# A hybrid decoder layer in float32: the order of high and low weight parts in the query and key projections

## The chip, the cores and the metric

The kernel runs on one core of a Trainium2 chip, as one launch. The metric is the device time of one execution in microseconds. The kernel before took 1053.3 us as the median of 3 runs (1052.99 to 1053.78). Engines are named as in the profile: PE is TensorE, DVE VectorE, ACT ScalarE, POOL GpSimd, SP the engine whose queue issues most DMAs.

## The reference

One decoder layer on x of 256 tokens by 2048 channels, all float32. The part that matters here is the token mixer:

```
h = rmsnorm(x, pre_mix_g)
q_a, k_a, v_a, q_b, k_b, v_b, f_b = split(h @ w_in)
o_a = swa_sink_attention(q_a, k_a, v_a, sinks)       # 16 query heads of 64, 2 key heads, window 128
o_b = forgetting_attention(q_b, k_b, v_b, cumsum(log_sigmoid(f_b + b_forget)))  # 16 heads of 64
x = x + rmsnorm(concat(rmsnorm(o_a), rmsnorm(o_b)) @ w_out, post_mix_g)
```

A channel mixer follows: an up-projection to 2 x 5632 columns, a causal convolution of width 3, GELU of one half times the other, a down-projection, a post-norm and a residual.

## The kernel before, in words

**Float32 as pairs.** TensorE multiplies operands that hold a rounded high part, and a low part carries the rest. A weight w is split by ScalarE (a cast to the high part, `w_split` or `w_high`, line 119) and VectorE (w minus high, the low part, line 122). The activations are held as `hT`: 16 slices of 128 channels, each 512 columns wide, 256 tokens' high parts and then their low parts. A product needs three terms: high weight by high and by low activations (one matmul of 512 columns, line 263), and low weight by high activations (one of 256 columns, line 270, added to the second half of the bank). The two halves of the bank are summed when it is evacuated (`evac_sum`, lines 448 to 450: a ScalarE copy, a VectorE add, a GpSimd multiply with the row norms), and the sum is split again into a high and a low part (`split`, lines 320 and 321).

**Projections with held weights.** `proj_T` computes 256 output columns of a weight matrix for all tokens, transposed, in two banks. The 2048 rows of the weight make four units of 512 rows. A unit is one load of 512 KB into one of 5 `raw` buffers, and one of 5 `wpair` buffers for its two parts. `get(u)` loads and splits a unit at its first use. `high(u)` issues 8 matmuls of 512 columns, `low(u)` 8 of 256. The argument `runs` is the order: its entries are, in turn, units whose high parts and units whose low parts are multiplied. After each unit of each run `tick()` is called, so a projection has eight ticks in either order. `w_parts` also sets where in the pair buffer the low part lies: `LOW[unit[0] % period[0]] * 4` columns behind column 1024, with `LOW = (14, 4, 4, 4)` and a period of 2 or 4 units.

**Who calls it.** In order of the program: two first projections written out by themselves (key and value of the SWA group, first query), three SWA query projections (`proj_T(w_in, g * 256, b2)`), the V projections of the FoX group (untransposed, line 317), then four times a FoX query projection and a FoX key projection. The second projection of `w_up` calls `proj_T` with an order of its own, `LONG`. All other projections of `w_up` use `proj_S` (line 300), in which every matmul has 256 columns.

**What sets the order of the work.** TensorE's order is the program's (`manual_schedule`). The attention of each pair of heads is hung into it by ticks: `later(n, f)` calls f at the n-th tick from now. `attend` hangs up four pieces, `tables`, `scores`, `transposes` and `pv`. For a SWA pair they come at the ticks of `stages(6 + 8 * g, m)`, for a FoX pair at those of `stages(5, m)`, that is 5, 9 + 4m and 13 + 4m ticks on, m being the pair's place in the projection (both pairs of a projection are scored at the same tick). `scores` (line 483) needs the split queries and keys and two banks of the attention pool, of which there are four; `transposes` (line 518) needs the softmax (lines 489 on VectorE, 501 on ScalarE, 508 on VectorE); `pv` (lines 527 and 529) needs the split probabilities `ph` and `pl`. Also hung on ticks: the transposition of the SWA values (`v_T`, tick 3, line 617; its split `vpa` frees its bank), and the cumulative sum of the forget gates (`cumsum`, tick 7 of the first FoX query projection), whose rows come back through DRAM as `cb` (line 582) for `tables`.

The order on ScalarE, VectorE, GpSimd and in SP's DMA queue is not written out in this part of the kernel; it is worked out when the program is built, from the program's order and from what is estimated to be ready. On the chip each of these queues runs in the order so fixed.

## Time and profile before

| | |
|---|---|
| median of 3 runs | 1053.3 us |
| the profiled execution | 1053.3 us |
| its span, first to last instruction | 1051.4 us |
| granted TensorE clock, mean | 0.997 |
| busy: PE, DVE, ACT, POOL | 1040.0, 837.2, 626.9, 166.5 us |
| `proj_T` with the default order | 32.7 to 73.3 us and 128.4 to 236.7 us |

How to read the lines. In a timeline a line gives start and length in us, the engine, the source line, the operation, what it writes and reads, the shape and how many instructions were merged; in brackets, the idle time of its engine before it and what ended that. Lengths of PE lines overlap, since matmuls are pipelined: the next line's start is where a stretch really ends. In the chain of waits a line gives start, length and the piece of work that the end of the program goes back to at that time. In the page's first part a line gives each engine's busy time, its share of the span and its instructions.

### The profile page before, as it was taken

The page shows a single profiled execution, that of the slowest core. Times are in us where ns is not written, and L with a number is a line of the kernel's source. Part 1 is how long each engine was busy: PE and PEld are TensorE (multiplying, and loading weights), DVE is VectorE, ACT ScalarE, POOL GpSimd, SP SyncE. Part 2 cuts the span into 40 slices and gives each one's busy share as a digit, 9 for nine tenths or more (in the row PEclk, how much of TensorE's full clock was granted, in tenths as well). Part 3 has the DMA queues.
Part 4 walks back from the last instruction along what each step waited for, and adds up shares of the span by engine and source line. Part 5 has one row for each costly group of instructions (what it writes and reads, how often), then busy time and mean ns, then how long its engine had stood idle before and what let it go on. Part 6 is the DMA issues. An engine that isn't in the chain of part 4 may idle for free.

```text
span 1051.4 us, 19021 instructions
## 1 busy us (share of the span) xinstructions
PE 1040.0 (99%) x7240; PEld 958.0 (91%) x7240; DVE 837.2 (80%) x1365; ACT 626.9 (60%) x1025; POOL 166.5 (16%) x210
## 2 busy tenths in 40 slices
PE   9999999999999999999999999999999999999996
PEld 7899988888888999999999888899999999988886
DVE  5999877887467888888877988967788777799783
ACT  6777757667557655555555655645565455566561
POOL 3253245441122210100000000000111000000023
PEclk9999999999999999999999999999999999999998
DMA  8645557555874878888875886777677776767783
GB/s 292 199 129 168 182 159 214 164 180 171 294 248 153 255 252 294 287 264 273 283 232 170 263 269 226 244 233 239 220 235 246 226 244 219 236 216 246 244 306 115
DMA packets 187335, 238.98 MB, mean 227 GB/s; under 512 B 8268, under 2 KB 154988, under 8 KB 186348
## 3 DMA queue, kind: packets, MB, share of 16 engines
q1 hardware_dynamic: 186924, 237.37, 69.5%
q8 instruction: 57, 0.93, 0.3%
q10 hardware_dynamic: 320, 0.40, 0.1%
q14 instruction: 34, 0.28, 0.1%
HBM read 221.86 MB, written 15.75 MB: 226 GB/s over the span
## 4 chain that ended last, share of the span: by engine, by line
PE 90%; DVE 4%; ACT 2%; DMA 1%; POOL 1%; issue 1%; SPq 0%; DVEq 0%; POOLq 0%; ACTq 0%
PE bank_att L300 23%; PE bank_acc L300 21%; PE bank_acc L1072 15%; PE bank_acc L317 12%; PE bank_acc L263 5%; PE bank_att L1072 5%; PE bank_acc L270 3%; DVE wpair L122 1%; PE bank_att L317 1%; POOL scr L450 1%; PE bank_att L518 1%; DMA raw<-in_w_in_dram 1%; PE bank_att L483 1%; PE bank_att L527 1%; DMA x_in<-in_x_dram 1%
## 5 line engine op out<-in xcount | busy, mean ns | idle before, releaser
L122 DVE TENSOR_TENSOR wpair<-raw,wpair 128x1024 fp32r<-128x1024 f32 (+3 forms) x317 | 383.6, 1225 | 116.9 <-ACT wpair L119 115.8
L119 ACT CAST wpair<-raw 128x1024 fp32r<-128x1024 f32 (+3 forms) x316 | 320.3, 1032 | 155.6 <-issue 62.6
L300 PE MATMUL bank_att<-hT,wpair 128*128 128x256 f32 x2112 | 241.2, 276 | 0.0
L300 PEld LDWEIGHTS bank_att<-hT,wpair 128*128 128x128 f32 x2112 | 240.4, 188 | 0.2
L300 PE MATMUL bank_acc<-hT,wpair 128*128 128x256 f32 x1920 | 219.2, 276 | 0.0
L300 PEld LDWEIGHTS bank_acc<-hT,wpair 128*128 128x128 f32 x1920 | 218.3, 188 | 0.0
L1072 PE MATMUL bank_acc<-wpair,G 128*128 128x512 f32 x636 | 153.5, 389 | 0.0
L1072 PEld LDWEIGHTS bank_acc<-wpair,G 128*128 128x128 f32 x636 | 119.1, 188 | 24.5
L263 PE MATMUL bank_acc<-hT,wpair 128*128 128x512 f32 x384 | 94.9, 394 | 0.0
L263 PEld LDWEIGHTS bank_acc<-hT,wpair 128*128 128x128 f32 x384 | 69.5, 188 | 13.2
L317 PE MATMUL bank_acc<-wpair,oT 128*128 128x512 f32 x336 | 78.0, 391 | 0.0
L317 PEld LDWEIGHTS bank_acc<-wpair,oT 128*128 128x128 f32 x336 | 62.6, 188 | 12.8
L1030 POOL TENSOR_TENSOR s<-yy 128x128 f32<-128x128 f32 x11 | 7.5, 681 | 408.1 <-DVE yy L1019 408.1
L320 ACT CAST wpair<-raw 128x1024 fp32r<-128x1024 f32 (+1 forms) x54 | 48.0, 892 | 36.2 <-PE bank_acc L1072 17.6
L321 DVE TENSOR_TENSOR wpair<-raw,wpair 128x1024 fp32r<-128x1024 f32 (+1 forms) x54 | 55.0, 1023 | 14.3 <-ACT wpair L320 13.4
L899 ACT ACTIVATE yy<-u,cw 128x256 f32<-128x256 f32 x88 | 48.4, 596 | 20.4 <-DVE u L894 15.3
L270 PE MATMUL bank_acc<-hT,wpair 128*128 128x256 f32 x384 | 49.4, 280 | 0.0
L270 PEld LDWEIGHTS bank_acc<-hT,wpair 128*128 128x128 f32 x384 | 47.4, 188 | 1.4
L317 PE MATMUL bank_acc<-wpair,hT 128*128 128x384 f32 (+1 forms) x288 | 47.7, 321 | 0.0
L317 PEld LDWEIGHTS bank_acc<-wpair,hT 128*128 128x128 f32 x288 | 45.4, 188 | 0.1
L320 ACT CAST G<-yy 128x256 fp32r<-128x256 f32 x44 | 16.0, 406 | 46.8 <-POOL yy L1031 23.9
L901 DVE SCALAR_TENSOR_TENSOR yy<-u,cw,yy 128x256 f32<-128x256 f32 x88 | 39.1, 482 | 2.4 <-ACT yy L899 2.2
(253 smaller groups left out, 1204.9 us busy)
## 6 DMA issues: line engine op xcount, KB each, us to landing
raw<-in_w_up_dram SPq DMA_DIRECT2D x176, 512.0 KB, 4.6
raw<-in_w_down_dram SPq DMA_DIRECT2D x68, 512.0 KB, 5.1
raw<-in_w_in_dram SPq DMA_DIRECT2D x51, 512.0 KB, 5.3
raw<-in_w_out_dram SPq DMA_DIRECT2D x32, 512.0 KB, 4.1
staged<-in_w_down_dram SPq DMA_DIRECT2D x44, 256.0 KB, 5.5
t_dram<-staged SPq DMA_DIRECT2D x22, 512.0 KB, 3.2
raw<-t_dram SPq DMA_DIRECT2D x14, 512.0 KB, 3.7
raw<-in_w_in_dram SPq DMA_DIRECT2D x16, 384.0 KB, 3.4
```

What stands on the lines that cost most here:

```text
L119: i1 = act.copy(hi[:, cs], raw[:, cs])
L122: i2 = dve.tensor_tensor(lo[:, cs], raw[:, cs], hi[:, cs].bitcast(F32), op=ALU.subtract)
L263: pe.matmul(b, hi[:, a, m * P:(m + 1) * P], hT[:, kt, 0:512], start=(kt == 0), stop=(last == (0, kt)))
L270: pe.matmul(b[:, 256:512], lo[:, a, m * P:(m + 1) * P], hT[:, u * 4 + a, 0:256], start=False, stop=(last == (1, u * 4 + a)))
L300: pe.matmul(b[:, m * 256:(m + 1) * 256], ws[:, a, m * P:(m + 1) * P], hT[:, kt, i * 256:(i + 1) * 256], start=not begun, stop=last == (low ...
L317: pe.matmul(b, a, r[:, cols], start=(first and i == 0), stop=(last and i == 2))
L320: act.copy(hi, src)
L321: dve.tensor_tensor(lo, src, hi.bitcast(F32), op=ALU.subtract)
L450: pool.tensor_tensor(dst, dst, row, op=ALU.mult)
L899: act.activation(y, u[:, 2:258], AF.Identity, bias=cw[:, 3, ch:ch + 1], scale=cw[:, 2, ch:ch + 1])
L901: dve.scalar_tensor_tensor(y, u[:, 1:257], cw[:, 1, ch:ch + 1], y, op0=ALU.mult, op1=ALU.add)
L1072: pe.matmul(b, x, r, start=b not in opened and not i, stop=closes and i == 2)
```

## The change

`proj_T` takes `LONG` as its default order. The high parts of units 0 and 1 still come first and their low parts next; then come the low parts of units 2 and 3, and their high parts last. The default order had the high parts of units 2 and 3 before their low parts. The period of the low parts' shift becomes 4 in every call (it was 2 in calls with the old default), so the low part of unit 2 is shifted by 16 columns instead of 56. The call for `w_up` passed `LONG` itself and now takes it as the default, so it stays as it is. The first start and the last stop of a bank's accumulation follow from the order: the last matmul of a bank is now a wide one.

```
-    def proj_T(w, c0, banks, runs=((0, 1), (0, 1), (2, 3), (2, 3))):
+    LONG = ((0, 1), (0, 1, 2, 3), (2, 3))
+
+    def proj_T(w, c0, banks, runs=LONG):
 
         parts, last = {}, ((len(runs) - 1) % 2, KT - 1)
-        unit[0], period[0] = 0, 4 if len(runs) == 3 else 2
+        unit[0], period[0] = 0, 4
...
-    LONG = ((0, 1), (0, 1, 2, 3), (2, 3))
...
-                    proj_T(w_up, DFF + c0, bv, LONG)
+                    proj_T(w_up, DFF + c0, bv)
```

## The prediction

> **What bounds the kernel now.** I read the page first, then the chain of waits, then TensorE's timeline over the stretch that the change touches (32 to 237 us), then VectorE's and ScalarE's timelines there.

> ```profile
> PE 1040.0 (99%) x7240; PEld 958.0 (91%) x7240; DVE 837.2 (80%) x1365; ACT 626.9 (60%) x1025; POOL 166.5 (16%) x210
> ...
> PE 90%; DVE 4%; ACT 2%; DMA 1%; POOL 1%; issue 1%; SPq 0%; DVEq 0%; POOLq 0%; ACTq 0%
> ```
> ```profile
> core 0: 1051.4 us, clock 0.997
> ```

> TensorE is busy 99% of the span and makes 90% of the chain. So time is won only where its stream gets shorter, and lost wherever it waits longer; it takes its matmuls in program order, so one that waits holds all behind it. The other engines matter where they are late. In this stretch I found it late only at the first scores and at the products with V in the FoX key projections (rows below). The profiled execution took 1053.3 us, as the median of the runs did; the 1.9 us around its span of 1051.4 are not touched.

> **The change.** Eleven projections run through `proj_T` with the default order: three SWA query ones, four FoX query, four FoX key ones. Each has eight steps with a tick after each: before H0 H1 L0 L1 H2 H3 L2 L3, after H0 H1 L0 L1 L2 L3 H2 H3 (H: 8 matmuls of 512 columns, L: 8 of 256). No instruction is added or removed. Three things follow: fewer turns between wide and narrow runs, other deadlines for the low parts, and, since attention pieces are hung on tick numbers, other places for those pieces in time.

> *Turns.* These runs stand without an attention piece between them (TensorE's timeline; start, length, source line), then a piece of the chain, two unbroken up-projections of matmuls of 256 columns:

> ```profile
> 143.35 3.82 PE L263 MATMUL bank_acc<-hT,wpair 128*128 128x512 f32 x16
> 147.01 2.00 PE L270 MATMUL bank_acc<-hT,wpair 128*128 128x256 f32 x16
> 148.85 3.82 PE L263 MATMUL bank_acc<-hT,wpair 128*128 128x512 f32 x16
> 152.51 2.00 PE L270 MATMUL bank_acc<-hT,wpair 128*128 128x256 f32 x16
> ...
> 381.14 21.76 PE bank_acc L300 x192
> ```

> Start to start, 16 wide take 3.66 us and 16 narrow 1.84. In the up-projections 192 matmuls take 21.76 us, 0.1133 each: 16 narrow would be 1.81, and 16 wide, twice the columns, 3.63. So each turn costs 0.03 us. A projection had four turns (the one from the projection ahead included) and keeps two: 2 x 0.03 saved, over about ten projections (the first one's saving falls into a wait, below) -0.6 us. A turn from or to an attention piece costs about the same for either kind of run, so those cancel.

> *The low parts' new deadline.* L2 and L3 come 3.66 us sooner. Are they split by then? Three rows: VectorE in the first projection and in the second FoX query projection, and TensorE in the second projection of `w_up`.

> ```profile
> 35.49 1.32 DVE L122 TENSOR_TENSOR wpair<-raw,wpair 128x1024 fp32r<-128x1024 f32 x1
> ```
> ```profile
> 154.77 1.30 DVE L122 TENSOR_TENSOR wpair<-raw,wpair 128x1024 fp32r<-128x1024 f32 x1 [3.18 <-ACT wpair L119]
> ```
> ```profile
> 352.71 2.98 PE L270 MATMUL bank_acc<-hT,wpair 128*128 128x256 f32 x24
> ```

> Counting the splits, the first row is the first projection's last low part, over by 36.81; L3 will want it near 39.6. In FoX the pairs run about five units ahead: the second row is the low part of unit 3 of the projection that runs from 154.4 to 167.6, over by 156.07 and due, after the change, near 162.9. No wait, and no cost; if the cover went, each late split would cost up to its 1.23 us. The pair of unit 2 comes free after H2, 0.9 us sooner than after L2. The low part's shift inside its pair (56 or 16 columns) changes for unit 2 alone; the `w_up` row ran with the new shifts and order already, 24 narrow ones in 2.98 us, normal but for the turn, so I cost it at nothing.

> *The first scores.* They hang on tick 6 of the first projection: before, behind H3; after, behind L3.

> ```profile
> 38.67 3.81 PE L263 MATMUL bank_acc<-hT,wpair 128*128 128x512 f32 x16
> 42.41 0.38 PE L483 MATMUL bank_att<-keys,qh 64*128 64x256 f32 x2
> ...
> 44.46 2.13 PE L270 MATMUL bank_acc<-hT,wpair 128*128 128x256 f32 x16
> 46.43 2.00 PE L263 MATMUL bank_acc<-hT,wpair 128*128 128x512 f32 x8
> ```
> ```profile
> 39.99 2.35 DVE L122 TENSOR_TENSOR wpair<-raw,wpair 128x1024 fp32r<-128x1024 f32 x2
> 42.37 0.87 DVE L321 TENSOR_TENSOR keys<-scr,keys 64x256 fp32r<-64x256 f32 x2
> 43.17 0.41 DVE L321 TENSOR_TENSOR vpa<-bank_att,vpa 128x256 fp32r<-128x256 f32 x1
> ```
> ```profile
> 40.59 0.40 ACT L320 CAST keys<-scr 64x256 fp32r<-64x256 f32 x1
> ```
> ```profile
> 43.63 0.90 PE bank_att L483 x9
> ...
> 69.90 1.53 PE bank_att L483 x23
> ```

> The 24 score matmuls take 2.05 us here (42.41 to 44.46), against 1.53 for the next group, which waits for nothing: they are already 0.5 us late. What they wait for: the keys' low half (VectorE, 42.37 on), and the value split of 43.17, over at 43.58, which frees the fourth attention bank; the chain takes them up again at 43.63. None of this depends on the order in the projection: it comes from the key and value evacuations, behind two weight splits of 2.35 us in VectorE's queue. After the change TensorE is at the scores at 38.67 + 1.84 + a turn, 40.6 us, and still leaves them at 44.46. Behind them stand then H2 and H3 (3.74 as from 38.67 to 42.41) where L2 and L3 stood (44.46 to 46.43, 1.97): +1.8 us. The bounds: 1.8 as the queue stands; 0.5 if value and key splits were served ahead of both weight splits, since then ScalarE's cast sets the time (40.59 + 0.40, and splits of 0.87 and 0.41: 42.3 instead of 43.6). I take 1.8, since nothing ahead of these splits has moved. The next scores, again at tick 6, two projections on, start later by this and earlier by their place, so keep their time near 69.9. The tightest piece left is a product in the first FoX query projection, behind L3 instead of H3:

> ```profile
> 138.94 0.40 PE L527 MATMUL bank_att<-ph,vpa 128*128 128x512 f32 x1
> ```
> ```profile
> 136.29 1.02 DVE L321 TENSOR_TENSOR pl<-bank_att,ph 128x384 fp32r<-128x384 f32 x2
> ```

> It comes 1.84 us sooner, at 137.1, its second matmul 0.23 later, and its low probabilities are there at 137.31: nothing, or 0.1.

> *Scores and products of the FoX group.* A pair of heads is scored at tick 5 of the next query projection, transposed at tick 1 of the key projection, multiplied with V at its tick 5. Tick 5 stood behind H2 and now stands behind L2: 0.92 us sooner. Everything else keeps its time. Does the softmax between follow? The third cycle:

> ```profile
> 190.15 0.38 PE L483 MATMUL bank_att<-keys,qh 64*128 64x256 f32 x2
> ...
> 191.68 2.09 PE L263 MATMUL bank_acc<-hT,wpair 128*128 128x512 f32 x8
> ...
> 201.64 2.00 PE L263 MATMUL bank_acc<-hT,wpair 128*128 128x512 f32 x8
> 203.48 0.62 PE L527 MATMUL bank_att<-ph,vpb 128*128 128x512 f32 x2
> 204.11 0.50 PE L527 MATMUL bank_att<-pl,vpb 128*128 128x512 f32 x1
> ...
> 230.95 0.62 PE L527 MATMUL bank_att<-ph,vpb 128*128 128x512 f32 x2
> 231.65 0.50 PE L527 MATMUL bank_att<-pl,vpb 128*128 128x512 f32 x1
> ```
> ```profile
> 189.71 2.36 DVE L122 TENSOR_TENSOR wpair<-raw,wpair 128x1024 fp32r<-128x1024 f32 x2 [0.59 <-ACT wpair L119]
> 192.10 0.42 DVE L489 CUSTOM_DVE_ANT_0 p<-bank_att,p 128x256 f32<-128x256 f32 x1
> ...
> 203.05 1.01 DVE L321 TENSOR_TENSOR pl<-bank_att,ph 128x384 fp32r<-128x384 f32 x2
> ...
> 217.25 2.36 DVE L122 TENSOR_TENSOR wpair<-raw,wpair 128x1024 fp32r<-128x1024 f32 x2 [0.58 <-ACT wpair L119]
> ```

> VectorE's first step on the scores (L489, 192.10) starts as two weight splits end (189.71 + 2.36); those wait for ScalarE casts that follow the evacuation of the key projection ahead, and those times do not move. So scores that end at 190.8 instead of 191.7 gain nothing; the softmax, the evacuation queued behind it on ScalarE and VectorE, and the low probabilities (203.05 + 1.01 = 204.06) come when they came. The third product with V, at 204.11, already waits for them; now TensorE reaches that piece 0.92 us sooner and waits as much longer, while H2, not L2, is still to do: +0.92. The fourth cycle is the same 27.5 us later (217.25, 231.65): +0.92. Bounds: above, 0.92 each, the move; below, the present waits gone, 0.2 each gained (204.11 - 203.48 and 231.65 - 230.95, less two matmuls of 0.23). I take 0.92, as the queue stands.

> The second cycle is otherwise:

> ```profile
> 162.40 1.05 ACT L119 CAST wpair<-raw 128x1024 fp32r<-128x1024 f32 x1 [1.63 <-DMA raw<-in_w_in_dram]
> ```
> ```profile
> 163.48 1.23 DVE L122 TENSOR_TENSOR wpair<-raw,wpair 128x1024 fp32r<-128x1024 f32 x1 [1.45 <-ACT wpair L119]
> 164.62 0.42 DVE L489 CUSTOM_DVE_ANT_0 p<-bank_att,p 128x256 f32<-128x256 f32 x1
> ```
> ```profile
> 153.04 3.62 SPq L582 DMA_DIRECT2D cb<-c_dram  x2
> 156.75 0.39 SPq L74 DMA_DIRECT2D raw<-in_w_in_dram  x1
> ```

> L489 stands behind a split (163.48) whose cast waited for a load; that load was issued at 156.75, behind the forget-gate rows (153.04) in SP's queue, and these go back to the cumulative sum on tick 7, now behind H2 instead of L2, 0.9 us sooner, as is the pair of unit 2. So the softmax moves with its place: 0 (bounds 0 and 0.92).

> *Sum:* -0.6 + 1.8 + 0.92 + 0.92 = +3.0 us. The rest of the span is TensorE without visible waits, apart from one tied to its own results, so a delay at 237 us reaches the end whole. 1053.3 + 3.0 = 1056.3.

> **Rivals.** *The queue is dealt anew* (0.26). VectorE's order is not written out here; it is worked out when the program is built, from what is ready. Tick 5 being 0.92 sooner, L489 may be put ahead of the second split (1.18 us) in cycles three and four. Against it: at 163.48 a split stood ahead although the scores were nearly done. Then the two 0.92 go: 1054.4, no measurable change; 0.2% is about what a measurement can tell.

> *Not slower: it is dealt anew before the first scores as well* (0.12). If the value and key splits come ahead of the splits of 39.99, the first scores lose 0.5 instead of 1.8: 1053.1. It decides at 41.1 us, where the second weight split starts; against it, nothing that goes into that queue so early has moved.

> *The second cycle does not follow* (0.09): its load or its cast keeps its time, +0.9: 1057.2.

> *The clock* (0.02). The granted clock is 0.997 over the span, but the warm-up matmuls show a slow head:

> ```profile
> 1.24 2.74 PE L174 MATMUL bank_acc<-junk 128*128 128x512 bf16 x6 [1.24 <-DVE junk L169]
> ```

> Six of 512 columns in 2.7 us are half the later pace. If the longer wait at 40.6 us brought such a stretch back, it would cost 1.3 us more: 1057.6. [...]

> **How the numbers follow.** The forecast has 0.46; its own range, from the sizes of its terms, is 1055.6 to 1057.0. With the first and third rival 0.81 is covered; the range 1053.6 to 1057.4 holds those and part of the second. Slower by over 0.2% (above 1055.4): forecast, second cycle, clock, 0.57. The same: 0.40. Faster (below 1051.2) would need more than all waits in this stretch and all turns: 0.03 for what I do not see.

> **What would show it.** Right: the first score group starts near 40.6 and ends near 44.5; the first projection ends 1.8 us later; the low-probability waits of cycles three and four grow to some 1.2 us; L489 still follows two splits; 32 narrow matmuls run in 3.65 us. Wrong: L489 ahead of a split there, score waits under 1 us, or a low run that waits for its split.

## The result, and the profile after

The kernel after takes 1061.3 us as the median of 6 runs (1060.1 to 1062.9), against 1053.2 for the kernel before (6 runs): 1.0075 times as long, 95% interval 1.0065 to 1.0085, so 8.1 us slower. The profiled execution took 1061.95 us, its span 1060.0. The prediction had the sign, but its 1056.3 us and its range, up to 1057.4, were too low.

From the page of the kernel after (engines' busy time; shares of the chain by engine), and its span and granted clock:

```profile
PE 1045.7 (99%) x7240; PEld 962.8 (91%) x7240; DVE 836.8 (79%) x1365; ACT 627.8 (59%) x1025; POOL 164.2 (15%) x210
...
PE 89%; DVE 4%; ACT 2%; DMA 2%; POOL 1%; issue 1%; SPq 0%; DVEq 0%; POOLq 0%; ACTq 0%
```
```profile
core 0: 1060.0 us, clock 0.992
```

TensorE is still busy 99% of the span. Yet with the same 7240 matmuls it is busy 5.7 us longer (1045.7 - 1040.0): a part of the loss is not waiting but slower matmuls, and the clock fell from 0.997 to 0.992. The page's shares would have hidden that; the mean clock shows it.

Where the 8.6 us of span were lost is read from the starts of the projections in TensorE's two timelines, matmul by matmul where a line merges the end of one projection with the start of the next. The first SWA query projection starts 0.1 us sooner than before, the next one 4.7 later (51.16 against 46.43). Then the distance stays: 4.6 at the end of the SWA projections, 4.6 and 4.7 at the first two FoX query projections (159.03 against 154.35). The second FoX key projection adds 3.7: the third query projection starts 8.4 later (190.03 against 181.67). From there to the end it is 8.3 to 8.6. So there are two places, and cycles three and four, where the prediction had put 1.84 us, are not among them.

**The first place.** TensorE's timeline of the kernel after at the first scores, and VectorE's (in the kernel after, L265 and L272 are the old L263 and L270):

```profile
40.51 0.83 PE L483 MATMUL bank_att<-keys,qh 64*128 64x256 f32 x2
...
42.76 0.38 PE L483 MATMUL bank_att<-keys,qh 64*128 64x256 f32 x2 [1.30 <-DVE keys L321]
...
45.01 8.13 PE L265 MATMUL bank_acc<-hT,wpair 128*128 128x512 f32 x24
53.07 0.24 PE L418 MATMUL bank_att<-ident,gst 32*128 32x32 f32 x1
```
```profile
42.28 0.87 DVE L321 TENSOR_TENSOR keys<-scr,keys 64x256 fp32r<-64x256 f32 x2
43.08 0.41 DVE L321 TENSOR_TENSOR vpa<-bank_att,vpa 128x256 fp32r<-128x256 f32 x1
```

The scores start at 40.51 (forecast 40.6), VectorE's queue stands as before, within 0.1 us, and the wait is the one forecast. But the 24 wide matmuls behind the scores (16 of this projection and 8 of the next) take 8.06 us from start to start (45.01 to 53.07); at the 3.63 per 16 of the prediction they take 5.45. The windows show why. Their columns: stretch, length, busy time and count of PE, PE's weight loads, DVE, ACT and POOL, granted clock, DMA share, GB/s:

```profile
38.00:41.00 3.00, 2.94 (x26) 2.61 (x24) 2.62 (x4) 2.24 (x5) 1.08 (x2) 1.00 0.84 282
41.00:45.00 4.00, 2.65 (x23) 2.12 (x23) 3.94 (x9) 1.65 (x3) 0.00 (x0) 0.79 0.64 189
45.00:50.00 5.00, 5.00 (x13) 3.93 (x13) 3.84 (x25) 4.57 (x18) 0.00 (x0) 0.50 0.54 170
50.00:60.00 10.00, 10.00 (x64) 8.68 (x63) 8.62 (x17) 5.68 (x12) 5.00 (x6) 0.99 0.27 79
...
170.00:179.00 9.00, 8.98 (x53) 7.61 (x52) 7.40 (x31) 6.92 (x22) 0.81 (x2) 1.00 0.47 162
179.00:182.00 3.00, 0.82 (x7) 0.63 (x7) 2.81 (x5) 1.74 (x5) 3.00 (x4) 1.00 0.79 242
182.00:187.00 5.00, 5.00 (x23) 4.44 (x24) 4.66 (x7) 3.85 (x8) 3.48 (x7) 0.66 0.62 201
```

At 45 to 50 us the clock is at exactly half: 13 matmuls are begun in 5 us. Read in windows of 0.1 us, the half clock lasts 6.83 us, from 43.32 to 50.15. A second such time lies in 182 to 187: 3.41 us, from 183.27. They begin 0.6 and 1.4 us behind the end of a wait of TensorE. In the kernel before the clock is 1.00 in each of these stretches. Of the 4.8 us that the first place costs (the 4.7, and 0.1 by which the first projection had started sooner), 1.8 is the wait that was forecast and about 3.0 the clock.

These times have a fixed length, and they lie on a grid. In the kernel after the clock falls at 43.32, at 183.27 and, at the program's end, at 1053.67. These are 139.95 and 870.40 us apart, which is 41 and 255 times 3.413 us, the length of one fall; the fall at the first scores lasts two lengths. In fox_interleaved, below, the clock falls in the third and the fourth FoX cycle at 207.9 and 238.6 us (worked out from granted clocks of 0.81 over 206 to 209 and 0.76 over 237 to 240): 30.7 apart, 9 times 3.413. Where the grid lies against the program differs: at the first scores the clock falls at 43.32 here and between 44.14 and 45.21 in three of the runs below (before_tick5 44.65, swa_only 45.21).

**The second place.** The products with V in the second FoX cycle, and in the third, in TensorE's timeline of the kernel after:

```profile
176.75 2.91 PE L272 MATMUL bank_acc<-hT,wpair 128*128 128x256 f32 x24
181.84 0.72 PE L527 MATMUL bank_att<-ph,vpb 128*128 128x512 f32 x2 [2.17 <-ACT ph L320]
...
182.85 0.39 PE L529 MATMUL bank_att<-ph,vpb 128*128 128x256 f32 x2
...
208.09 2.91 PE L272 MATMUL bank_acc<-hT,wpair 128*128 128x256 f32 x24
210.94 0.72 PE L527 MATMUL bank_att<-ph,vpb 128*128 128x512 f32 x2
...
211.97 0.40 PE L529 MATMUL bank_att<-ph,vpb 128*128 128x256 f32 x2
```

The second cycle in the kernel before:

```profile
175.62 0.74 PE L527 MATMUL bank_att<-ph,vpb 128*128 128x512 f32 x2
176.63 0.50 PE L527 MATMUL bank_att<-pl,vpb 128*128 128x512 f32 x1 [0.27 <-DVE pl L321]
176.97 0.39 PE L529 MATMUL bank_att<-ph,vpb 128*128 128x256 f32 x2
```

In the second cycle TensorE now waits 2.17 us for the probabilities' high part. Counted from the end of the narrow run (181.84 - 2.17 = 179.67) to the next operation (182.85), the three wide products take 3.18 us; before, from 175.62 to 176.97, 1.35. That is 1.8 more, and half clock for 3.4 us costs another 1.7: 3.5 of the 3.7. In the third cycle they take 1.03 (210.94 to 211.97), against 0.97 before (203.48 to 204.45).

### The profile page after: what moved, and what is told of

Read it like the earlier page. It is cut to its first block, busy times and chain, and to the rows that moved or that the text cites. A ratio compares the mean times of both kernels' runs of the same rounds, so it can differ in the third digit from the quotient of the medians.

```text
span 1060.0 us, 19016 instructions
## 1 busy us (share of the span) xinstructions
PE 1045.7 (99%) x7240; PEld 962.8 (91%) x7240; DVE 836.8 (79%) x1365; ACT 627.8 (59%) x1025; POOL 164.2 (15%) x210
## 4 chain that ended last, share of the span: by engine, by line
PE 89%; DVE 4%; ACT 2%; DMA 2%; POOL 1%; issue 1%; SPq 0%; DVEq 0%; POOLq 0%; ACTq 0%
PE bank_att L300 23%; PE bank_acc L300 21%; PE bank_acc L1072 15%; PE bank_acc L317 11%; PE bank_acc L265 6%; PE bank_att L1072 5%; PE bank_acc L272 3%; DVE wpair L122 1%; PE bank_att L317 1%; PE bank_att L483 1%; PE bank_att L527 1%; PE bank_att L518 1%; DMA raw<-in_w_in_dram 1%; ACT p L501 1%; POOL scr L450 1%
## 5 line engine op out<-in xcount | busy, mean ns | idle before, releaser
L122 DVE TENSOR_TENSOR wpair<-raw,wpair 128x1024 fp32r<-128x1024 f32 (+3 forms) x317 | 383.2, 1223 | 121.7 <-ACT wpair L119 120.7
L119 ACT CAST wpair<-raw 128x1024 fp32r<-128x1024 f32 (+3 forms) x316 | 320.6, 1033 | 157.0 <-issue 62.1
L300 PE MATMUL bank_att<-hT,wpair 128*128 128x256 f32 x2112 | 241.2, 276 | 0.0
L300 PEld LDWEIGHTS bank_att<-hT,wpair 128*128 128x128 f32 x2112 | 240.4, 188 | 0.2
L300 PE MATMUL bank_acc<-hT,wpair 128*128 128x256 f32 x1920 | 219.2, 276 | 0.0
L300 PEld LDWEIGHTS bank_acc<-hT,wpair 128*128 128x128 f32 x1920 | 218.3, 188 | 0.0
L265 PE MATMUL bank_acc<-hT,wpair 128*128 128x512 f32 x384 | 94.8, 401 | 0.0
L265 PEld LDWEIGHTS bank_acc<-hT,wpair 128*128 128x128 f32 x384 | 72.6, 194 | 14.7
L320 ACT CAST wpair<-raw 128x1024 fp32r<-128x1024 f32 (+1 forms) x54 | 48.0, 892 | 35.4 <-PE bank_acc L1072 17.0
L321 DVE TENSOR_TENSOR wpair<-raw,wpair 128x1024 fp32r<-128x1024 f32 (+1 forms) x54 | 55.0, 1024 | 13.6 <-ACT wpair L320 12.7
L272 PE MATMUL bank_acc<-hT,wpair 128*128 128x256 f32 x384 | 49.4, 284 | 0.0
L272 PEld LDWEIGHTS bank_acc<-hT,wpair 128*128 128x128 f32 x384 | 47.1, 191 | 0.9
L320 ACT CAST G<-yy 128x256 fp32r<-128x256 f32 x44 | 16.0, 405 | 46.8 <-POOL yy L1031 23.9
```

Source lines behind the costliest of these rows:

```text
L119: i1 = act.copy(hi[:, cs], raw[:, cs])
L122: i2 = dve.tensor_tensor(lo[:, cs], raw[:, cs], hi[:, cs].bitcast(F32), op=ALU.subtract)
L265: pe.matmul(b, hi[:, a, m * P:(m + 1) * P], hT[:, kt, 0:512], start=(kt == 0), stop=(last == (0, kt)))
L272: pe.matmul(b[:, 256:512], lo[:, a, m * P:(m + 1) * P], hT[:, u * 4 + a, 0:256], start=False, stop=(last == (1, u * 4 + a)))
L300: pe.matmul(b[:, m * 256:(m + 1) * 256], ws[:, a, m * P:(m + 1) * P], hT[:, kt, i * 256:(i + 1) * 256], start=not begun, stop=last == (low ...
L320: act.copy(hi, src)
```

## The experiments

The theories after reading the two traces. *Clock*: a wait of some 1.3 to 2.2 us halves TensorE's clock for a stretch of 3.4 us or two. *Second cycle*: the weight load behind the forget-gate rows in SP's queue comes later, by itself and not as a consequence of the SWA part. Rivals: the new order itself makes the wide matmuls slower; the delay in the SWA part shifts the loads of the FoX part. The ratios stand with their intervals against the kernel before on the same chip:

| run | median us | ratio (95%) |
|---|---|---|
| swa_only | 1056.6 | 1.0026 (1.0017 to 1.0035) |
| fox_only | 1057.3 | 1.0034 (1.0021 to 1.0046) |
| before_tick5 | 1056.9 | 1.0032 (1.0021 to 1.0043) |
| filled_wait | 1059.2 | 1.0048 (1.0033 to 1.0063) |
| rows_by_pool | 1058.0 | 1.0039 (1.0026 to 1.0052) |
| scores_tick7 | 1058.0 | 1.0041 (1.0028 to 1.0054) |
| tick7_and_pool | 1055.6 | 1.0020 (1.0011 to 1.0028) |
| fox_h3_first | 1057.3 | 1.0034 (1.0021 to 1.0048) |
| fox_interleaved | 1060.2 | 1.0064 (1.0050 to 1.0077) |
| kept_times | 1051.4 | 0.9980 (0.9971 to 0.9989) |

### One part alone: swa_only and fox_only

The old order, with its period of 2, for the calls of one group; `TURNS` is the old default.

```
 swa_only:
-  proj_T(w_in, 1280 + g * 256, bq)          +  proj_T(w_in, 1280 + g * 256, bq, TURNS)
-  proj_T(w_in, 2304 + g * 256, bk)          +  proj_T(w_in, 2304 + g * 256, bk, TURNS)
 fox_only:
-  proj_T(w_in, g * 256, b2)                 +  proj_T(w_in, g * 256, b2, TURNS)
```

> The new order in the three SWA projections alone; the FoX ones as before. Clock theory: 1.8 of wait and about 3 of half clock, less 0.1 for the turns: about 1057.8 us, and no further slow clock. Wait-only theory: 1054.9. If the second cycle's wait comes from the SWA group: 1061.

> The new order in the eight FoX projections alone; the three SWA ones as before. Clock theory with a second cause in the FoX group: no wait at the first scores and no slow clock there, so 3.6 us of loss stay at the product of the second cycle (1.9 wait, 1.7 clock) less 0.5 for the turns: about 1056.3 us. If the second cycle was late only because of what happened in the SWA group: 1052.7 us. Long-run theory: a slow clock in each of eight projections.

TensorE's timeline of swa_only at the first scores:

```profile
43.41 0.39 PE L484 MATMUL bank_att<-keys,qh 64*128 64x256 f32 x2 [1.23 <-DVE keys L322]
```

Each part alone is slower. In swa_only the wait at the first scores (1.23 us) is followed by half clock from 45.21 to 48.63, and the second cycle has no wait. In fox_only the first scores are undisturbed and the second cycle waits 2.18 us again: that wait needs nothing of the SWA part, and the rival by which the loads are shifted falls. In the profiled execution of fox_only the clock stayed up after it; this execution (1056.2 us) was also the fastest of its six by 0.9 us.

Swa_only's ten runs tell more than their median. They lie in groups: four at 1054.9 to 1055.2, four at 1056.5 to 1057.0, then 1058.1 and 1059.3. The mean clock of the groups is 0.998, 0.996 to 0.997, and 0.994 in the last two. Half clock for 3.41 us costs 1.7. So the same program seems to meet none, one or two such stretches from execution to execution. The profiled one, at 1056.5, had one. The lowest group is 1.4 us above the kernel before (1053.6): close to the forecast of 1.8 for the wait less 0.2 for three projections' turns.

### The early scores without the new order: before_tick5

In the kernel before, the first scores are hung one tick sooner, behind H2; nothing else moves.

```
-  stages(6 + 8 * g, m))
+  stages(6 + 8 * g, m) if g else (5, 10 + 4 * m, 14 + 4 * m))
```

> The kernel before, its order of projections untouched, with only the first scores hung on tick 5 instead of tick 6, that is 1.84 us sooner. Clock theory: the same wait of about 2.4 us, the same fall of the clock: 1053.2 + 1.8 + 3.2 = about 1058.2 us. Wait-only theory: 1055.0. Long-run theory: no run of 32 narrow ones here, so no fall of the clock, 1055.0 at most.

TensorE's timeline and the windows of this run:

```profile
42.77 0.38 PE L483 MATMUL bank_att<-keys,qh 64*128 64x256 f32 x2 [1.30 <-DVE keys L321]
```
```profile
41.00:45.00 4.00, 2.64 (x25) 2.07 (x26) 3.94 (x9) 1.67 (x3) 0.00 (x0) 0.96 0.65 195
45.00:48.00 3.00, 3.00 (x9) 2.35 (x9) 2.49 (x18) 2.78 (x12) 0.00 (x0) 0.50 0.86 258
```

The same wait of 1.30 us and the same fall of the clock, in the old order of matmuls. The rival that the new order slows the wide matmuls falls. I had expected two stretches as in the kernel after; there was one, of 3.41 us from 44.65; and the median is 1.3 us under the 1058.2 that I had forecast.

### The wait kept but filled: filled_wait

The kernel after, with 24 matmuls of 128 columns on scratch data put ahead of the first scores, into columns of the bank that nothing reads. The scores wait for the same keys; TensorE is busy meanwhile. This adds work and leaves none out. TensorE's timeline and the windows follow the expectation.

```
+                if j == 0:
+                    for _ in range(24):
+                        pe.matmul(sb[0][:, 384:512], junk[:, 0:P], junk[:, 0:P],
+                                  start=True, stop=True)
```

> The changed kernel with 24 idle matmuls (128 columns of zeros into the unused columns of a score bank) put ahead of the first scores, to keep TensorE busy in its wait. Clock theory: the 2.4 us wait at the first scores made the clock fall to half from about 43 to 50 us; with the wait filled the clock stays at 1.00 there, the scores still end near 44.5 us, the high parts behind them run in 3.7 us, and the kernel takes 1061.3 - 3.2 = about 1058.1 us. Wait-only theory (the lost time is the waits themselves): no change, 1061.3. Long-run theory (32 narrow matmuls in a row, or the new shifts of the low parts, make the slow stretch): no change, and the half clock stays.

```profile
41.72 1.51 PE L481 MATMUL bank_att<-junk 128*128 128x128 bf16 x24
...
44.08 0.38 PE L487 MATMUL bank_att<-keys,qh 64*128 64x256 f32 x2 [0.30 <-DVE keys L321]
```
```profile
41.00:45.00 4.00, 3.64 (x47) 3.10 (x47) 3.94 (x7) 2.93 (x5) 0.00 (x0) 1.00 0.52 166
45.00:48.00 3.00, 3.00 (x21) 2.54 (x22) 2.85 (x12) 1.63 (x8) 0.00 (x0) 1.00 0.91 257
```

The keys come when they came, the visible gap is 0.30 instead of 1.30, and the clock stays at 1.00. The next projection starts 3.0 us later than before, and this one had started 1.2 later in this execution: 1.8 lost in it, the forecast term alone. The second cycle still waits 2.18 us, with half clock behind it. Adding 24 matmuls made the kernel 2.1 us faster than the kernel after by the medians, 2.8 by the ratios; forecast were 3.2. That the idle time brings the half clock is shown: idle put in (before_tick5) brings it, idle filled takes it away. The other profiled executions agree: at the first scores the clock fell in all four that wait 1.2 to 1.3 us there (the kernel after, swa_only, before_tick5, rows_by_pool), and in none of the eight others.

### The second cycle: rows_by_pool

What holds the load? SP's queue, ScalarE, VectorE and GpSimd in the kernel after, a fence each:

```profile
157.76 4.68 SPq L582 DMA_DIRECT2D cb<-c_dram  x2
162.54 17.86 SPq L74 DMA_DIRECT2D raw<-in_w_in_dram  x8
```
```profile
168.26 1.05 ACT L119 CAST wpair<-raw 128x1024 fp32r<-128x1024 f32 x1 [2.66 <-DMA raw<-in_w_in_dram]
```
```profile
158.54 1.45 DVE L122 TENSOR_TENSOR wpair<-raw,wpair 128x1024 fp32r<-128x1024 f32 x1 [2.24 <-ACT wpair L119]
...
160.63 1.23 DVE L122 TENSOR_TENSOR wpair<-raw,wpair 128x1024 fp32r<-128x1024 f32 x1
...
169.34 1.23 DVE L122 TENSOR_TENSOR wpair<-raw,wpair 128x1024 fp32r<-128x1024 f32 x1 [2.49 <-ACT wpair L119]
170.48 0.42 DVE L489 CUSTOM_DVE_ANT_0 p<-bank_att,p 128x256 f32<-128x256 f32 x1
```
```profile
157.37 0.37 POOL L589 TENSOR_SCALAR p<-cb,cq 128x128 f32<-128x128 f32 x1
...
158.90 1.33 POOL L589 TENSOR_SCALAR p<-cb,cq 128x128 f32<-128x128 f32 x1
...
160.68 1.42 POOL L589 TENSOR_SCALAR p<-cb,cq 128x128 f32<-128x128 f32 x1
```

The weight load is issued at 162.54, 3.5 us after the projection's start at 159.03; before it was 2.4 (156.75 against 154.35). So it came 1.1 later in its place, where I had it 0.9 sooner. It stands behind two loads of forget-gate rows, which wait until GpSimd has read the rows before them from the same buffers: the second is issued at 162.12, and GpSimd's operation of 160.68 ends at 162.10. GpSimd's operations of 128 columns take 0.37 us, but 1.33 and 1.42 where a weight split runs on VectorE (158.54 and 160.63); three operations in this chain are so stretched (the third, of 256 columns, at 154.22: 2.35 us where others take 0.48), two before (154.98 and, at the head, 149.83). Both splits started first (158.54 and 160.63), and both GpSimd operations end 0.24 us behind them, at 160.23 and 162.10. What holds these operations up was not tested here by itself.

The experiment takes the row loads out of SP's queue:

```
-                sp.dma_start(cb.rearrange("p e k -> p (e k)"),
+                pool.dma_start(cb.rearrange("p e k -> p (e k)"),
```

> The changed kernel with the loads of the forget-gate rows (cb) issued from GpSimd's queue instead of SP's, so that no weight load stands behind them. Theory: in the second FoX cycle the softmax is late since a weight load waited in SP's queue for the tables on GpSimd (162.5 us, 1.1 us later than before beside the same projection), which ran over by 1.3 us where VectorE's weight splits lay beside them. With the load free the 2.2 us wait at the product near 180 us and the slow clock behind it go: 1.9 + 1.7 less, about 1057.7 us. Rival (the softmax is late for the tables themselves, or by the place of the scores alone): the wait stays, 1061.3.

TensorE's timeline at the second cycle's products:

```profile
178.76 0.72 PE L527 MATMUL bank_att<-ph,vpb 128*128 128x512 f32 x2 [0.94 <-ACT ph L320]
```

L489 now starts 10.0 us after the projection's start instead of 11.45, the wait is 0.94 instead of 2.17, and the clock stays up there. The queue position is worth 1.2 us of the wait. The rest of it is the earlier deadline (0.92) with a softmax that starts only 0.27 sooner than before (10.27).

### Later scores, and both mends: scores_tick7, tick7_and_pool

The kernel after with the first scores on tick 7, so behind H2, and then with GpSimd's row loads as well.

```
-  stages(6 + 8 * g, m))
+  stages(6 + 8 * g, m) if g else (7, 10 + 4 * m, 14 + 4 * m))
```

> The changed kernel with the first scores hung on tick 7, behind the high parts of unit 2, which is the time they had before. Theory: no wait beyond the old 0.5 us at the first scores, no slow clock there; what stays is the second FoX cycle, so about as fox_only less 0.15 for the turns: 1057.0 us (ratio 1.0033). If the SWA group loses elsewhere too: above 1058.

> The changed kernel with both: the first scores on tick 7 and the rows loaded from GpSimd's queue. If the two waits are all of the loss, only the turns are left, and the old waits of the products may shrink: 1052.5 to 1053.2 us, within 0.1% of before. If something else is lost in the new order: above 1055.

The wait and the half clock at the first scores are gone in both. Scores_tick7 keeps the second cycle's wait (2.17 us) with half clock behind it; in tick7_and_pool no half clock is left in the stretch. It still missed its expected time, by new waits that I had not counted: the first pair's product, still on tick 14, is now too early for its softmax and waits 0.76 us (0.75 in scores_tick7), and the products of the second and fourth cycle wait 0.87 and 0.72. Ten of tick7_and_pool's eleven runs lie within 1055.4 to 1055.8: three waits of under 0.9 us brought no steps of 1.7.

### Why cycles three and four cost nothing: fox_h3_first, fox_interleaved

L489 starts 9.5 us after the query projection's start there (199.56 against 190.03); before it was 10.4 (192.10 against 181.67). What I had called fixed has moved. ScalarE's timelines, before and after, at the head of that chain:

```profile
180.96 1.06 ACT L119 CAST wpair<-raw 128x1024 fp32r<-128x1024 f32 x1 [0.45 <-PE bank_acc L270]
```
```profile
188.42 1.05 ACT L119 CAST wpair<-raw 128x1024 fp32r<-128x1024 f32 x1 [1.78 <-PE bank_acc L265]
```

The cast writes into a pair buffer, and TensorE's last use of that buffer ends its wait: a narrow run (L270) before, a wide one (L265) after. Against the query projection's start (181.67, 190.03) that is 0.71 ahead before and 1.61 ahead after: 0.9 sooner, and behind this cast stand on ScalarE and VectorE the evacuation, the key splits, the two weight splits, and L489. To test this, the FoX calls (the SWA ones in the old order) were to free a pair later: first H3 ahead of H2, then the two units' high parts taken in turn, slice by slice, so that no pair is free until the end.

```
 fox_h3_first:
+    SWAP = ((0, 1), (0, 1, 2, 3), (3, 2))
 fox_interleaved, for the run of units 2 and 3:
+                for a in range(4):
+                    for u in us:
+                        hi, kt = get(u)[0], u * 4 + a
...
+                    if a in (1, 3):
+                        tick()
```

> As fox_only, but with the high parts of unit 3 ahead of those of unit 2 in each FoX projection, so that the pair of unit 2 comes free at the end of the projection: 1.83 us later than in fox_only and 0.92 later than in the kernel before. Theory: cycles three and four cost nothing in the changed kernel because the cast for the next pair, released by unit 2, and all behind it on ScalarE and VectorE came 0.9 us sooner. Then here they come later, and the products of these two cycles wait 1 to 2 us each: 2 to 4 us above fox_only (1057.2), more if the clock falls. Rival (the softmax follows the scores, whatever is released): like fox_only.

> As fox_only, but the high parts of units 2 and 3 are taken in turn, four rows of one and four of the other, so that no pair comes free before the last half microsecond of a projection (in fox_only one comes free 1.8 us before its end). Theory: cycles three and four cost nothing in the changed kernel since the cast that waits for this pair, and behind it the evacuation of the keys, two weight splits and the softmax, came 0.9 us sooner than before. Then here that cast comes about 1.3 us later than in fox_only and the products of cycles three and four wait about 1 us more each: 1057.2 + 2 = 1059.3 us or more. Rival (that release does not matter): as fox_only, 1057.2.

Fox_h3_first tells nothing apart: the cast came 1.62 us ahead of the start, as in fox_only, so with the end of H3, which is now the first of the two wide runs; a pair came free as early as before. In fox_interleaved (ScalarE, VectorE, TensorE; L500 is the old L489):

```profile
183.07 1.05 ACT L119 CAST wpair<-raw 128x1024 fp32r<-128x1024 f32 x1 [2.33 <-PE bank_acc L283]
```
```profile
193.89 0.42 DVE L500 CUSTOM_DVE_ANT_0 p<-bank_att,p 128x256 f32<-128x256 f32 x1
```
```profile
183.32 1.98 PE L266 MATMUL bank_acc<-hT,wpair 128*128 128x512 f32 x8
...
206.78 0.50 PE L538 MATMUL bank_att<-pl,vpb 128*128 128x512 f32 x1 [2.00 <-DVE pl L332]
...
237.75 0.51 PE L538 MATMUL bank_att<-pl,vpb 128*128 128x512 f32 x1 [2.02 <-DVE pl L332]
```
```profile
209.00:213.00 4.00, 4.00 (x18) 3.46 (x17) 1.81 (x4) 0.88 (x3) 2.83 (x6) 0.72 1.05 359
```

The cast comes 0.25 us ahead of the start (183.07 against 183.32), L500 10.6 after it, and the products of cycles three and four wait 2.0 us each, each time followed by a time at half clock. So the release of the pair carries the softmax. The waits are longer than the 1.2 of the prediction; what the remaining 0.8 is I did not trace.

### The order with the old times: kept_times

Does the order itself cost anything? The kernel after, with each attention piece that had come sooner hung one tick later, so that as much of the projection is done ahead of it as before (tick 6 is then behind L3, tick 7 behind H2):

```
+  at = list(stages(6 + 8 * g, m))
+  for i, k in enumerate(at):
+      at[i] += (g * 8 + k) in (6, 14, 22, 66)
+  swa_pair(2 * g + m, q_pair(b2[m]), tuple(at))
...
-  fox_pair(2 * g + m, qs[m], ki, stages(5, m))
+  fox_pair(2 * g + m, qs[m], ki, stages(5, m) if g == 3 else (6, 14, 17) if m else (6, 9, 14))
```

> The changed kernel with every attention piece of the touched projections hung one tick later where the new order made its tick earlier (tick 5 to 6, 6 to 7 and the like), so that each piece keeps the time it had; the cumulative sum stays on tick 7. If the loss is only that pieces came sooner than their inputs, the turns alone are left: 1053.5 - 0.6 = about 1052.9 us, the waits as before and no slow clock in the middle. If the order itself costs something (the splits' load on VectorE beside GpSimd's tables, an earlier release of a pair): a wait near the second FoX cycle stays, 1054 to 1057.

```profile
core 0: 1049.7 us, clock 0.998
```
```profile
171.90 3.81 PE L272 MATMUL bank_acc<-hT,wpair 128*128 128x256 f32 x32
175.54 0.63 PE L527 MATMUL bank_att<-ph,vpb 128*128 128x512 f32 x2
...
176.24 0.40 PE L529 MATMUL bank_att<-ph,vpb 128*128 128x256 f32 x2
...
202.58 0.63 PE L527 MATMUL bank_att<-ph,vpb 128*128 128x512 f32 x2
...
203.28 0.40 PE L529 MATMUL bank_att<-ph,vpb 128*128 128x256 f32 x2
```

This is faster than both: 0.998 times the kernel before, 2.1 us, and all of its interval is below 1. The span is 1.7 us shorter. The three wide products take 0.70 us in every cycle (175.54 to 176.24, 202.58 to 203.28), where before they took 1.35, 0.97 and, in the fourth, 1.04: 0.65 + 0.27 + 0.34 = 1.3 us of old waiting gone, because the earlier release of the pairs brings the softmax sooner while the products keep their place. The remaining 0.4 is about what the turns had been forecast to save. In the second cycle SP's order came out otherwise here, with weight loads between the two row loads, and L489 starts 8.9 us after the projection's start; so for that cycle the two causes are not separated.

## Why the prediction was wrong

- *Turns, -0.6*: right in mechanism. The 32 narrow matmuls take 3.65 us (after, 151.72 to 155.37), as forecast. In the kernel after some 0.3 of it is eaten by 0.1 and 0.2 of new waits in cycles three and four; kept_times is shorter by 0.4 that no wait accounts for.
- *Low parts' deadline, 0*: right; no narrow run waits for a split.
- *First scores, +1.8*: right, in the start, in what ended the wait and in the size (filled_wait: 1.8). The scores end at 45.01 and not at 44.5, since the clock is already down.
- *The clock* (a rival at 0.02, priced at 1.3 us): this failed first. In the profiled execution there were three stretches of 3.41 us at half clock, 3 x 1.7 = 5.1 us of the 8.6 if TensorE was busy throughout them. I took the price from six matmuls at the head, while a fall lasts a whole stretch of 3.41 us or two. The chance of 0.02 was my estimate, and nothing in the trace before bears on it: TensorE's longest wait behind the head there is 0.7 us. That is a reason for a wide range and not for a small chance. The runs show falls behind waits of 1.23, 1.30 and 2.17 us.
- *Second cycle, 0, "the softmax moves with its place"*: failed. The load came 1.1 us later in its place, not 0.9 sooner; with the earlier deadline it cost 1.8 us, twice the upper bound and twice the price of the rival for it (0.09, +0.9). I had followed SP's queue back to the row loads, but not to the GpSimd operations that these wait for, and not to what slows those.
- *Cycles three and four, 0.92 each, "those times do not move"*: failed. They moved by 0.9 us with the release of a pair. The prediction says itself that the pair of unit 2 comes free 0.9 us sooner, and uses it for the second cycle; it did not follow this into the casts ahead of L489. The measured cost is 0.1 and 0.2.
- *The queue dealt anew* (0.26): not what happened in the kernel after. VectorE's L489 still follows the two splits; the whole queue came sooner.

Without its three slow stretches the profiled execution would be near 1061.95 - 5.1 = 1056.8 us. That this is close to 1056.3 is chance: two terms of 0.92 were wrong, and a third, put at 0, was 1.8.

What stays open: what a wait must be to bring the clock down. In these executions a fall begins at the end of the stretch of 3.413 us of the grid that holds the wait or most of it: in the kernel after the waits end at 42.76 and 181.84, the stretches at 43.32 and 183.27. In all ten falls ahead of the program's end TensorE had idled 1.28 us or more within that stretch; stretches with 0.94 us or less brought none, and the wait of 1.09 us in fox_interleaved's second cycle was split over two, 0.84 and 0.24. But in the profiled execution of fox_only a stretch with 1.72 us of idle time (its wait of 2.18 us lay across the end of a stretch) brought no fall (clock 1.00 from 172 to 188 us), so idle time alone does not decide it. The kinds of matmul in these stretches differ, and that was not tested. Nor is it shown why the kernel after had two lengths of half clock at the first scores where before_tick5, swa_only and rows_by_pool had one. Only there did the fall begin 1.7 us ahead of the end of the scores; in the other three it began at most 0.2 us ahead of it, or behind it.

## What to carry to other kernels

When pieces hang on a count of steps, reordering the steps moves them in time; move the count with the order, and look for a gain only then. Cost a new wait of TensorE not by its length alone but by what its clock does afterwards, 1.7 us for each stretch here, and where a trace has no such wait, let the range hold it. A buffer's release is a time like any other: follow it through each queue whose head waits for it, as far as the step that you call fixed.
